# First-layer attention: the first three heads' projections and rotary embedding ahead of their share of the S5 table work

## Chip, cores and metric

One NeuronCore of a Trainium2 chip runs the whole program in one launch. The metric is the device time of one execution in microseconds. The kernel before was timed in three runs; their median is 2292.32 us.

## What is computed

Two transformer-like blocks of two layers each, on 256 latent and 256 context tokens of width 1024. The first layer of the first block is windowed attention with rotary embedding, 16 query heads and 4 key heads of width 128; the second is an S5 state-space mixer. All data are float32. What matters here, cut from the reference:

```python
pz = h @ w_in; pzc = hc @ w_in          # layer 0: q (16x128), k (4x128), v (4x128), z (2048)
q = rope_2d(q, row, col); k = rope_2d(k, row, col)      # latent tokens only
pr = softmax_with_sink(concat([s_win, s_ctx], -1), sink)
...
y_attention * silu(z) @ w_out            # end of layer 0
...
abar = exp(lam * dt); bbar = ((abar - 1) / lam)[..., None] * bmat    # layer 1: S5, two directions
hs = associative_scan(abar, bbar u);  y = einsum('btgp,gnp->btgn', hs, cmat).real
```

The S5 layer's input-independent tables (powers of `abar`, `bbar`, `cmat` in a transposed layout, and what is built from them) are computed by this kernel during the attention layer, as work beside the heads.

## The kernel before, in words

Every float32 matrix product is done as three passes (`mm3`, lines 197 to 202): each operand is split into a high part, rounded by ScalarE (`copy_a`, line 149), and a low part, the difference, mostly on VectorE (`sub`, line 152). A weight unit (`wunit`, line 204) is one 512 KB load on SyncE's queue into a ring of six staging tiles `st`, the high part on ScalarE and the low part on VectorE into a ring of three tiles `wl`.

`block1_l0` (line 622) makes the modulated inputs `hT`, the value projection of all heads, and then calls `l0_attention` (line 415). In it

- `heads(h)` (line 449) makes, for every fourth head, the key projection and its rope, and for each head the q projection with rope and the gate projection z. One projection is one weight unit and 8 times `mm3`, 24 matmuls, into one of three PSUM tiles `pa`. `rope` (line 431) reads that tile: ScalarE copies (line 149), VectorE differences (line 152), two matmuls with a rotation matrix (lines 437, 438), and products with cos and sin (line 158); only then is the tile `pa` free, for the projection that comes three later. The result is one tile `h` (a ring of 16, line 120), kept until the head's scores.
- `scores(h)` (line 461) and `values(h)` (line 506) are the attention of one head.
- `side` is a list of four generators: the S5 tables `s5_transposed` (line 763), the modulation `ada`, `s5_build_w` on GpSimd (line 951), `s5_build_v` on VectorE (line 901). One `next` does one step.

`s5_transposed` is driven in the lead alone, in 22 steps. Step 1 makes four transposes (line 768) and four VectorE copies. Step 2 is `s5_tables` (line 844): chains of small VectorE multiplications (`cmul`, lines 836 to 838; `three`, lines 841, 842), ScalarE copies into the tile `P` (line 867), and two `pwd` and five `apd` stores on GpSimd's queue. Steps 3 to 10 load the c matrices (two tiles `h` of 512 KB per real or imaginary part) and transpose them with 128-row matmuls (line 804), evacuated by VectorE and ScalarE in turn (lines 807 to 809) into four tiles `h`, which go to DRAM as `cbd` on GpSimd's queue. Steps 11 to 18 do the same for b, and steps 19 to 22 multiply b by the factor `qt` (lines 820 to 828) and store it.

The order on each engine's queue is not the order of the program: the framework plans it at compile time (line 2057, `schedule_with_timeline_sim=True`), taking on each engine the earliest instruction of the program that its plan has ready, and each engine then executes its queue strictly in that order. So the order of the program is a ranking.

Of the kernel before, what the change touches and what calls it, by code (L numbers as in the profile page):

```python
# [110 lines left out]
class Builder:  # L111
# [303 lines left out]
    def l0_attention(self, hT, vps, W, sink, negsink, Wo, gates, ada):  # L415
# [8 lines left out]
        def proj(n0):  # L424
            ps = self.pacc()
            w = self.w_ws(W, n0)
            for kt in range(8):
                self.mm3(ps, w[kt], (hT[kt][:, 0, :], hT[kt][:, 1, :]), kt == 0, kt == 7)
            return ps

        def rope(ps):
            hl = self.hslot(F32R)[:, :].rearrange("p (a b) -> p a b", a=2)
            pr = self.qslot(F32R)[:, :].rearrange("p (a b) -> p a b", a=2)
            self.split(pr, ps[:, :256])
            self.split(hl[:, :, 256:], ps[:, 256:])
            rq = self.pms()
            nc.tensor.matmul(rq[:, :256], self.rot, pr[:, 0, :], start=True, stop=False)
            nc.tensor.matmul(rq[:, :256], self.rot, pr[:, 1, :], start=False, stop=True)
            t = self.qslot()
            self.mul(t[:, :256], ps[:, :256], self.c["cos1"])  # L440
            self.mul(t[:, 256:], rq[:, :256], self.c["sin1"])
            self.add(t[:, :256], t[:, :256], t[:, 256:], self.off)
            self.split(hl[:, :, :256], t[:, :256], lo_eng=self.off)
            return hl
# [4 lines left out]
        def heads(h):  # L449

            g = h // 4
            if h % 4 == 0:
                Ks[g] = rope(proj(2048 + g * 128))
            q = rope(proj(h * 128))
            zps = proj(3072 + h * 128)
            th = self.qslot()
            nc.scalar.activation(th, zps, AF.Tanh, scale=0.5)
            self.stt(th, th, 1.0, zps, ALU.add, ALU.mult)
            pend[h] = [q, th]
# [136 lines left out]
        LEAD = 3  # L596
        side = [self.s5_transposed(), ada, self.s5_build_w(), self.s5_build_v()]
        for h in range(LEAD):
            for _ in range((2, 10, 10)[h]):
                next(side[0], None)  # L600
            heads(h)
        scores(0)
        for h in range(16):
            if h < 15:
# [1456 lines left out]
```

## Time and profile before

| what | value |
|---|---|
| median of three runs | 2292.32 us (2291.62 to 2294.66) |
| profiled execution, its own time | 2306.04 us |
| its span, first to last instruction | 2304.3 us |
| TensorE (PE) busy | 87% of the span |
| VectorE (DVE) / ScalarE (ACT) / GpSimd (POOL) busy | 62% / 38% / 32% |

All times of the trace are microseconds from the start of the span. Each engine's row in a timeline gives start, duration, engine, line of the code and operation, the tile written and the tiles read, and in brackets the idle time of the engine ahead of it and what ended it. The attention layer runs from about 57 to 700 us.

### The profile page before, as it was taken

The numbers are of one execution on the slowest core, as the hardware profiler recorded it, in microseconds if no ns is written. First come the engines' busy times: TensorE is split into PE (matmuls) and PEld (weight loads), VectorE is DVE, ScalarE is ACT, GpSimd is POOL, SyncE is SP. The second block draws the span as 40 slices with busy tenths as digits, with TensorE's granted clock in tenths as the row PEclk, the third lists the DMA queues.
The fourth block names the chain that finished last, engine by engine and source line by source line (L and its number), as shares of the span: only waits on it lengthen the run. The fifth ranks groups of instructions, "written<-read, shape, count | busy, mean of one in ns | idle before, by whom it ended". The sixth has DMA issues, their size and how long they took to land. (4 is left out here: it accounts for less than half of the span.)

```text
span 2304.3 us, 34637 instructions
## 1 busy us (share of the span) xinstructions
PE 2014.0 (87%) x13236; PEld 1587.5 (69%) x13236; DVE 1426.6 (62%) x2948; ACT 875.3 (38%) x1650; POOL 744.2 (32%) x498
## 2 busy tenths in 40 slices
PE   6697777999988878659998899999999989888998
PEld 3574555667767766647886565778888877557997
DVE  5788887766784867654656636553333476355556
ACT  2233233343534443443544243342222243334443
POOL 1686887900003201223442200121211513112334
PEclk9798877999999899779999879999999999788999
DMA  8566535554646666978675407433233225364663
GB/s 267 172 193 206 172 107 158 151 164 146 221 158 132 189 158 191 219 203 264 181 255 173 158 2 253 140 97 96 83 109 92 88 73 189 119 193 125 191 187 120
DMA packets 362775, 368.56 MB, mean 160 GB/s; under 512 B 27512, under 2 KB 291420, under 8 KB 362608
## 3 DMA queue, kind: packets, MB, share of 16 engines
q1 hardware_dynamic: 356048, 355.32, 51.7%
q0 software_dynamic: 2208, 6.29, 1.0%
q10 hardware_dynamic: 4352, 4.72, 0.6%
q8 instruction: 105, 1.72, 0.3%
q14 instruction: 62, 0.51, 0.1%
HBM read 319.62 MB, written 46.65 MB: 159 GB/s over the span
## 5 line engine op out<-in xcount | busy, mean ns | idle before, releaser
L149 ACT ACTIVATE wl<-st 128x1024 fp32r<-128x1024 f32 (+1 forms) x328 | 340.6, 1043 | 479.9 <-issue 177.6
L152 POOL TENSOR_TENSOR wl<-st,wl 128x1024 fp32r<-128x1024 f32 (+1 forms) x95 | 232.3, 2446 | 839.4 <-ACT wl L149 816.5
L152 DVE TENSOR_TENSOR wl<-st,wl 128x1024 fp32r<-128x1024 f32 (+1 forms) x233 | 312.0, 1341 | 242.5 <-ACT wl L149 240.8
L200 PE MATMUL pa<-h,wl 128*128 128x512 f32 (+1 forms) x1152 | 404.7, 354 | 13.9 <-ACT wl L149 6.5
L201 PE MATMUL pa<-h,wl 128*128 128x512 f32 (+1 forms) x1152 | 404.6, 352 | 0.0
L202 PE MATMUL pa<-h,wl 128*128 128x512 f32 (+1 forms) x1152 | 402.1, 351 | 1.1 <-DVE wl L152 1.1
L200 PEld LDWEIGHTS pa<-h,wl 128*128 128x128 f32 x1152 | 221.3, 193 | 49.7 <-ACT wl L149 8.3
L202 PEld LDWEIGHTS pa<-h,wl 128*128 128x128 f32 x1152 | 221.6, 193 | 31.0 <-DVE wl L152 1.7
L201 PEld LDWEIGHTS pa<-h,wl 128*128 128x128 f32 x1152 | 222.2, 193 | 27.5 <-issue 0.2
L201 PE MATMUL pa<-wl,h 128*128 128x512 f32 (+1 forms) x528 | 211.5, 401 | 11.2 <-DVE wl L152 9.8
L200 PE MATMUL pa<-wl,h 128*128 128x512 f32 (+1 forms) x528 | 206.0, 403 | 8.2 <-ACT h L149 4.1
L202 PE MATMUL pa<-wl,h 128*128 128x512 f32 (+1 forms) x528 | 203.2, 396 | 6.5 <-POOL h L152 5.6
L152 POOL TENSOR_TENSOR h<-q,h 128x256 fp32r<-128x256 f32 (+2 forms) x82 | 96.5, 1184 | 236.2 <-ACT h L149 162.3
L168 DVE SCALAR_TENSOR_TENSOR q<-q,pa 128x512 f32<-128x512 f32 (+1 forms) x104 | 59.0, 568 | 168.6 <-ACT q L1888 92.5
L149 ACT ACTIVATE h<-pm 128x512 f32<-128x512 f32 (+3 forms) x182 | 92.8, 546 | 153.7 <-PE pm L1556 38.9
L201 PE MATMUL pm<-wl,h 128*128 128x512 f32 (+1 forms) x376 | 146.7, 393 | 2.7 <-DVE wl L152 2.0
L299 PE MATMUL pf<-st,cs 128*32 128x512 f32 x576 | 97.0, 702 | 54.6 <-DMA st<-in_w_ada_dram 28.8
L202 PE MATMUL pm<-wl,h 128*128 128x512 f32 (+1 forms) x376 | 142.5, 391 | 0.0
L200 PE MATMUL pm<-wl,h 128*128 128x512 f32 (+1 forms) x376 | 140.1, 393 | 0.9 <-ACT wl L149 0.9
L201 PEld LDWEIGHTS pa<-wl,h 128*128 128x128 f32 x528 | 105.1, 199 | 38.0 <-DVE wl L152 11.5
L200 PEld LDWEIGHTS pa<-wl,h 128*128 128x128 f32 x528 | 104.1, 198 | 38.9 <-ACT h L149 8.5
L202 PEld LDWEIGHTS pa<-wl,h 128*128 128x128 f32 x528 | 103.6, 197 | 30.0 <-POOL h L152 6.4
(360 smaller groups left out, 3814.6 us busy)
## 6 DMA issues: line engine op xcount, KB each, us to landing
st<-in_w_ada_dram SPq DMA_DIRECT2D x96, 512.0 KB, 4.8
st<-in_ada_w_dram SPq DMA_DIRECT2D x48, 512.0 KB, 5.7
st<-in_w_ffn_gate_dram SPq DMA_DIRECT2D x44, 512.0 KB, 4.6
st<-in_w_ffn_up_dram SPq DMA_DIRECT2D x44, 512.0 KB, 3.9
st<-in_w_ffn_down_dram SPq DMA_DIRECT2D x44, 512.0 KB, 3.7
st<-in_attn_w_in_dram SPq DMA_DIRECT2D x40, 512.0 KB, 4.3
st<-in_w_out_dram SPq DMA_DIRECT2D x40, 512.0 KB, 4.0
wd<-w SPq DMA_DIRECT2D x64, 256.0 KB, 4.0
```

What stands on the lines that cost most here:

```text
L149: self.nc.scalar.activation(o, i, AF.Copy)
L152: return (eng or self.nc.vector).tensor_tensor(o, a, b, op=ALU.subtract)
L168: self.nc.vector.scalar_tensor_tensor(o, a, s, b, op0=op0, op1=op1)
L200: mm(o, w[0], x[0], start=start, stop=False)
L201: mm(o, w[0], x[1], start=False, stop=False)
L202: mm(o, w[1], x[0], start=False, stop=stop)
L299: mm = nc.tensor.matmul(ps[32 * q:32 * q + 32, :], self.cs[:, blk, kt, :, :], st[:, (q % 2) * 512:(q % 2 + 1) * 512], start=k0 == 0, stop= ...
```

## The change

In the loop over the first three heads, `heads(h)` stands ahead of that head's steps of `s5_transposed` (2, 10 and 10 of them) and no longer behind them. Nothing is added or removed.

```diff
         LEAD = 3
         side = [self.s5_transposed(), ada, self.s5_build_w(), self.s5_build_v()]
         for h in range(LEAD):
+            heads(h)
             for _ in range((2, 10, 10)[h]):
                 next(side[0], None)
-            heads(h)
         scores(0)
```

## Rows read from the trace of the kernel before

**Rows 1.** The page: the span, and the busy time of each engine.
```profile
span 2304.3 us, 34637 instructions
PE 2014.0 (87%) x13236; PEld 1587.5 (69%) x13236; DVE 1426.6 (62%) x2948; ACT 875.3 (38%) x1650; POOL 744.2 (32%) x498
```
**Rows 2.** Stretches A:B, their length, busy us of each engine, granted clock, DMA.
```profile
75.00:400.00 325.00, 256.57 (x1491) 185.98 (x1490) 280.61 (x358) 106.00 (x238) 242.21 (x166) 0.83 0.54 167
400.00:640.00 240.00, 234.51 (x1513) 173.39 (x1512) 172.03 (x282) 103.69 (x221) 58.12 (x40) 0.97 0.54 174
72.00:126.00 54.00, 40.31 (x200) 30.06 (x199) 53.33 (x74) 15.71 (x27) 32.22 (x27) 0.84 0.54 163
126.00:150.00 24.00, 24.00 (x210) 20.73 (x209) 17.20 (x38) 10.99 (x29) 21.93 (x19) 1.00 0.92 289
150.00:215.00 65.00, 48.14 (x253) 31.96 (x251) 64.41 (x71) 17.41 (x43) 52.15 (x33) 0.90 0.58 176
...
102.00:110.00 8.00, 1.40 (x4) 0.63 (x3) 8.00 (x10) 1.32 (x3) 5.24 (x5) 0.50 0.80 260
```
**Rows 3.** Timeline of PE in the lead.
```profile
76.55 0.50 PE L200 MATMUL pa<-h,wl 128*128 128x512 f32 x1
...
93.48 1.06 PE L299 MATMUL pf<-st,cs 128*32 128x512 f32 x8
101.63 0.58 PE L437 MATMUL pm<-q,rot 128*128 128x256 f32 x1 [7.09 <-ACT q L149]
104.05 0.58 PE L438 MATMUL pm<-q,rot 128*128 128x256 f32 x1 [1.84 <-DVE q L152]
...
109.97 0.77 PE L200 MATMUL pa<-h,wl 128*128 128x512 f32 x1 [4.65 <-DVE q L158]
...
113.51 0.39 PE L202 MATMUL pa<-h,wl 128*128 128x512 f32 x1
```
**Rows 4.** Timeline of ACT in the lead.
```profile
98.63 2.55 ACT L149 ACTIVATE h<-h 64x512 f32<-64x512 f32 x4 [5.79 <-DVE h L155]
101.20 0.38 ACT L149 ACTIVATE q<-pa 128x256 fp32r<-128x256 f32 x1
```
**Rows 5.** Timeline of DVE.
```profile
58.45 0.28 DVE L163 TENSOR_SCALAR a<-pm 128x128 f32<-128x128 f32 x1
...
72.09 1.58 DVE L152 TENSOR_TENSOR wl<-st,wl 128x1024 fp32r<-128x1024 f32 x1 [13.36 <-ACT wl L149]
...
79.05 1.27 DVE L841 COPY h<-h 128x128 f32<-128x128 f32 x1
...
86.89 0.21 DVE L841 COPY h<-h 128x128 f32<-128x128 f32 x1
...
109.42 0.41 DVE L158 TENSOR_TENSOR q<-pa,cst 128x256 f32<-128x256 f32 x1
109.75 0.41 DVE L155 TENSOR_TENSOR h<-h 128x256 f32<-128x256 f32 x1
...
359.93 1.53 DVE L155 TENSOR_TENSOR q<-q 128x256 f32<-128x256 f32 x1
```
**Rows 6.** POOL: its first S5 product on the timeline, and all products of `w`.
```profile
60.95 1.51 POOL L158 TENSOR_TENSOR w<-bs,qg 128x512 f32<-128x512 f32 x1 [20.47 <-DMA bs<-in_s_b_im_dram]
...
L155 POOL TENSOR_TENSOR w<-w,wd x64: 1267/1590/2170, 65.1 to 456.5; 128x512 f32<-128x512 f32 x64
```
**Rows 7.** SyncE's queue: the loads of b.
```profile
127.31 1.04 SPq L146 DMA_DIRECT2D h<-in_s_b_re_dram  x2
...
139.24 5.68 SPq L146 DMA_DIRECT2D h<-in_s_b_im_dram  x2
```
**Rows 8.** PE: the transposing matmuls of c and b.
```profile
122.26 4.97 PE L804 MATMUL pm<-cst,h 128*64 128x128 f32 x64
...
132.70 7.33 PE L804 MATMUL pm<-cst,h 128*64 128x128 f32 x96
```

## The prediction

> **What bounds the kernel now.** The page first, for the scale: TensorE is busy in 87% of the span, VectorE in 62% [rows 1]. A change to the first three heads must be read from its own stretch, so next the stretches. From 400 to 640 us PE is busy in 234.5 of 240 us and VectorE in 172: there PE sets the pace, and whatever earlier stretches lose or win passes on to the end one for one. From 75 to 400 us it is the reverse: VectorE is busy in 280.6 of 325 us and PE in 256.6 [rows 2]. The lead, where the change works, is the fullest part of that: 53.3 of 54 us on VectorE from 72 to 126, then 17.2 of 24, then 64.4 of 65 [rows 2]. The reader should see that PE's idle time in the lead is mostly a consequence: it waits for a VectorE that has no time to spare, except in the 24 us from 126 to 150, where PE is the full one (24.0 of 24) and VectorE has 6.8 us over.
>
> Then the timeline of PE. From 76.55 to 93.48 it makes 72 matmuls, the projections K0, q0 and z0, at 0.235 us each. Then, but for 1.06 us of other work, it stands: 7.09 us until ScalarE has split K0, 1.84 us for a VectorE difference, 4.65 us until VectorE's product with the cosine gives back K0's tile `pa`, for which q1's projection waits [rows 3]. Together 13.6 us. ScalarE's timeline says why: K0's projection ended about 82.2 (76.55 plus 24 times 0.235), but its split runs at 101.20, behind four copies of the S5 table `P` which themselves waited 5.79 us for VectorE's table chain [rows 4]. The cosine product comes at 109.42 [rows 5]. So the ranking of tables ahead of heads is really felt: rope K0 stands some 20 us behind table work in two in-order queues.
>
> **The change, part by part.** No work is added or removed; every term is a displacement.
>
> Heads(0) ahead of two steps of tables. K0's split no longer ranks behind the copies of `P`, and its six VectorE operations at 0.41 us [rows 5], 2.5 us, no longer rank behind the chain. They would run soon after 82.2, and q1 would find its tile free at 93.5. On PE this takes away up to 13.6 us of standing. The granted clock also fell to 0.50 in 102 to 110, its 1.2 GHz level, and a matmul at 109.97 took 0.77 us where one at 113.51 took 0.39 [rows 2, 3]; the 3.5 us between them would be 1.8 at the full clock, so PE's side could give 15.4 us at most.
>
> What VectorE lets through of that. The same table, rope and weight operations are still due before scores(0), and VectorE is full in 72 to 126 and in 150 to 215 [rows 2]. PE running ahead lets VectorE start rope and weight work earlier but shortens none of it. What it can fill is the 6.8 us that VectorE has over in 126 to 150: there PE, at work on projections and the c and b transposes at once, made it wait; with q1 and z1 out of the way earlier that wait goes. The bounds of the gain are 0 (the hole stays) and 15.4 us (all of PE's standing goes for good, which needs holes elsewhere: from 75 to 400 us VectorE has 44.4 in all [rows 2]). I take 6.8, the hole itself, as it is the nearest row, in the lead and on the engine that is full.
>
> The moved steps' other instructions. Step 1's four transposes and copies, done by 58.7 now, have VectorE's hole from there to 72.09 as cover, 13.4 us [rows 5], and being ready early they should stay in it: 0; without that cover they cost under 2 us. The table stores on POOL's queue (two `pwd`, five `apd`) get later by the 2.5 us of each rope that passes them; what is queued behind them is POOL's product stream, which runs to 456.5 us [rows 6] and which no head waits for: 0. The c and b loads on SyncE's queue (four tiles each) now rank behind the weight loads of heads(1) and heads(2); on PE the 256 transposing matmuls they feed have projections to run beside: 0 for the queue itself, but see the third rival. The b products and their `cbd` stores rank behind heads(2), by two weight differences and one rope; the only readers of `cbd`, the loads of `s5_build_v`, rank behind values(0) in both versions. VectorE's total up to scores(0) stays as it is, so 0 for the order alone, with the b products still the last work ahead of scores(0). ScalarE is busy in 15.7 of 54 us [rows 2]: 0.
>
> The products on VectorE and POOL touch each other. The same small copy took 1.27 us at 79.05, beside POOL's products, and 0.21 us at 86.89 [rows 5]; rope's addition took 0.41 at 109.75 and the same form 1.53 at 359.93 [rows 5]. I take no change of the sum, as the table operations that change places with rope are of the kind that is stretched too. The Trainium skill, "SBUF — State Buffer", section "Summary: rules for kernel authors", says that a VectorE operation with two SBUF inputs and a GpSimd operation that reads SBUF block each other whole, and to schedule whichever is off the critical path; by that rule the change puts ropes into POOL's busiest stretch, and only the ropes' price would count, which the fourth rival works out from the rows.
>
> The sum against the profiled execution: 2306.0 us less 6.8 is 2299.2. That execution is 13.7 us above the median of the three runs (2292.3), and its span is 1.7 below its own time. The forecast in terms of the median is 2292.3 less 6.8, or 2285.5; I say 2286.
>
> **The rivals.** First, nothing comes of it: VectorE stays full, PE's 13.6 us turn up again ahead of the b products and scores(0), where it already has only 48.1 of 65 us of work [rows 2]. For it: VectorE's 53.3 of 54. The same time comes out if the change does not do what it says, since the planner ranks and does not obey: POOL's first S5 product runs at 60.95 [rows 6], though the program has it behind values(0). Against it: K0's split truly stood behind the `P` copies. Time: 2292.
>
> Second, the larger gain: PE stays ahead, and the rest of VectorE's 44.4 us of holes up to 400 us takes up what the lead could not. Then 15.4 us go and the time is 2277. Against it: PE can run ahead by three `pa` tiles only, and scores and values follow VectorE.
>
> Third, slower: the ring of 16 tiles `h` becomes the bound. The b loads go out at 127.31, just when the first 64 transposing matmuls, of c's real part, have ended at 127.23 and given back two tiles [rows 7, 8]: the ring is full now. With q1 and q2 held from earlier on, the b loads would wait for the next two tiles, those of c's imaginary part, free after 64 of the 96 matmuls from 132.70 on, 132.70 + 64 x 0.0764 = 137.6 [rows 8]. That is 10.3 us later for the loads, for the b products behind them and for scores(0) behind those; it decides from the point where the displaced ropes and tables no longer fill VectorE meanwhile. Nothing gained and 10.3 lost is 2302.6. For it: the imaginary b load already takes 5.68 us to issue [rows 7]. Against it: c may start earlier when PE is ahead, and VectorE has its displaced table work to do meanwhile.
>
> Fourth, the ropes pay for POOL: four ropes (K0, q0, q1, q2) with two SBUF-only operations each, stretched by 1.53 less 0.41, cost 8 x 1.12 = 9.0 us, of which the gain of 6.8 covers most: 2294.5. By the skill's rule above this is the price of the change; rows of rope at 0.41 us in the lead speak against its full size.
>
> **How the numbers follow.** About 0.2%, 4.6 us, is what a measurement of this kernel can tell from no change. The forecast at 2286 has a chance of 0.34, the larger gain 0.11; nothing 0.20 and the ropes beside POOL 0.08, both within 4.6 us; the full ring 0.27. That gives faster 0.45, same 0.28, slower 0.27. Cases of both signs hold most of the chance; the likeliest one's own range is 2282 to 2290, from half as much again to a third of the term. The range reaches to the larger gain's 2277 and nearly to the ring's full price: 2277 to 2302, which leaves out about half of the first and a third of the second, some 15 in 100.
>
> **What would show it.** Right: K0's split on ScalarE runs within a few us of 82 and ahead of the second `P` copies; PE has no hole of 7 us between 93 and 102, and q1 follows z0 directly; VectorE stays full up to 150 and on, with its 6.8 us gone; scores(0) come some 7 us earlier, and PE's idle time from 75 to 400 us, 68.4 now, is smaller by as much. Wrong: the same sum of PE's idle time in that stretch in other places (the first rival); b loads later than 127 with VectorE idle ahead of the b products (the third); rope's additions at 1.2 us or more in the lead (the fourth). If the stretch up to 400 us keeps its time and the total still moves, the plan has changed further down, and the reasoning here does not reach it.

## The result, and the profile after

The change made the kernel slower: 2308.3 us, median of four runs, against 2291.97 us for the kernel before beside it, a ratio of 1.0067 with a 95% interval of 1.0046 to 1.0088. That is 16.3 us slower, where the forecast had some 6 us faster, and 6 us above the range's end. The page of the changed kernel:

```profile
span 2309.4 us, 34623 instructions
...
PE 2001.0 (87%) x13236; PEld 1582.4 (69%) x13236; DVE 1428.1 (62%) x2948; ACT 876.1 (38%) x1650; POOL 748.5 (32%) x498
```

The work is the same as in [rows 1]. The two spans differ by 5.1 us only, since the profiled execution of before is 13.7 us above its median, as the prediction's sum says. So the spans are no measure here; I read the stage the change is in. Its first and last marks are the first scores (line 472) and the last statistics of the attention's output (line 593). These are groups of instructions by line: count, shortest/mean/longest ns, first start and last end. Kernel before:

```profile
L472 PE MATMUL pm<-lowneg,identb x16: 229/230/331, 166.3 to 645.4; 128*128 128x128 bf16 x16
...
L593 DVE BATCH_NORM_STATS2 bn<-h x8: 680/690/695, 684.3 to 696.8; 128x6 f32<-128x512 f32 x8
```

Changed kernel:

```profile
L472 PE MATMUL pm<-lowneg,identb x16: 229/230/330, 195.1 to 661.8; 128*128 128x128 bf16 x16
...
L593 DVE BATCH_NORM_STATS2 bn<-h x8: 639/684/695, 698.0 to 710.8; 128x6 f32<-128x512 f32 x8
```

The first scores come 28.8 us later (195.1 less 166.3), the end of the attention 14.0 us later (710.8 less 696.8), near the 16.3 of the medians. In this pair of profiles more than the kernel's loss is made before the first scores, and about half of it comes back on the way.

Now the lead itself, the stretch from about 57 us to the first scores. The stretches of the changed kernel (columns as in [rows 2]):

```profile
57.00:100.00 43.00, 39.16 (x167) 31.14 (x166) 19.63 (x27) 14.18 (x24) 39.58 (x27) 0.96 0.60 165
...
100.00:150.00 50.00, 31.04 (x172) 22.68 (x171) 48.96 (x67) 11.89 (x19) 33.84 (x28) 0.80 0.60 186
126.00:150.00 24.00, 18.01 (x114) 14.65 (x114) 23.54 (x34) 4.48 (x8) 16.51 (x15) 0.80 0.75 237
150.00:215.00 65.00, 42.74 (x296) 34.66 (x294) 50.38 (x74) 15.46 (x44) 48.45 (x36) 0.84 0.68 212
...
75.00:400.00 325.00, 229.19 (x1434) 171.80 (x1435) 276.38 (x348) 100.08 (x229) 251.35 (x170) 0.83 0.52 162
...
57.00:215.00 158.00, 112.93 (x632) 88.49 (x630) 118.98 (x166) 41.53 (x87) 121.86 (x89) 0.86 0.63 191
```

and two of the kernel before that [rows 2] do not have:

```profile
57.00:100.00 43.00, 31.94 (x134) 24.24 (x132) 29.04 (x39) 12.95 (x21) 28.94 (x22) 0.88 0.54 153
...
57.00:215.00 158.00, 121.85 (x693) 89.97 (x691) 136.40 (x186) 48.00 (x105) 117.35 (x86) 0.88 0.63 192
```

Between 57 and 100 us PE is busier than before, 39.2 us against 31.9, and yet the lead is lost. Over 57 to 215 VectorE does 119.0 us of work instead of 136.4: the engine that was full in the lead stood 17.4 us longer, and not all of it in one place. Up to 100 us it does 9.4 us less (19.6 instead of 29.0). From 100 to 150 it does 6.0 more (49.0 instead of 43.0, which is 136.40 less 29.04 and less the 64.41 of [rows 2]), nearly all of that in 126 to 150, where it is now busy in 23.5 of 24 us and was in 17.2. From 150 to 215 it does 14.0 less (50.4 instead of 64.4). So there are two losses, one before 100 us and a larger one after 150.

The first loss, on three timelines. PE of the changed kernel:

```profile
74.88 0.50 PE L200 MATMUL pa<-h,wl 128*128 128x512 f32 x1
...
92.18 0.38 PE L768 MATMUL pm<-cst,ab 128*128 128x128 f32 x2
92.40 0.38 PE L768 MATMUL pm<-cst,qg 128*128 128x128 f32 x2
92.54 0.48 PE L200 MATMUL pa<-h,wl 128*128 128x512 f32 x1
...
124.89 0.58 PE L437 MATMUL pm<-q,rot 128*128 128x256 f32 x1 [6.73 <-ACT q L149]
...
158.41 9.01 PE L804 MATMUL pm<-cst,h 128*64 128x128 f32 x64 [7.20 <-DMA h<-in_s_c_im_dram]
```

PE of the kernel before, the same four transposes:

```profile
56.99 0.40 PE L768 MATMUL pm<-cst,ab 128*128 128x128 f32 x2
57.22 0.38 PE L768 MATMUL pm<-cst,qg 128*128 128x128 f32 x2
```

VectorE of the changed kernel:

```profile
70.44 1.81 DVE L152 TENSOR_TENSOR wl<-st,wl 128x1024 fp32r<-128x1024 f32 x1 [11.99 <-ACT wl L149]
77.27 1.23 DVE L152 TENSOR_TENSOR wl<-st,wl 128x1024 fp32r<-128x1024 f32 x1 [5.02 <-ACT wl L149]
81.23 0.42 DVE L152 TENSOR_TENSOR q<-pa,q 128x256 fp32r<-128x256 f32 x1 [2.73 <-ACT q L149]
...
89.63 1.52 DVE L152 TENSOR_TENSOR h<-q,h 128x256 fp32r<-128x256 f32 x1
...
92.61 1.34 DVE L155 TENSOR_TENSOR q<-q 128x256 f32<-128x256 f32 x1
93.88 0.41 DVE L770 COPY q<-pm 128x256 f32<-128x256 f32 x1
...
95.40 1.16 DVE L858 COPY h<-a 128x128 f32<-128x128 f32 x1
...
165.26 0.38 DVE L809 COPY h<-pm 128x128 f32<-128x128 f32 x1 [9.12 <-ACT h L149]
```

and of the kernel before, the first operation of the table chain (the serial run of small operations in step 2):

```profile
73.60 1.31 DVE L858 COPY h<-a 128x128 f32<-128x128 f32 x1
```

The four transposes of step 1 ran at 57 us before. In the changed kernel they stand in PE's queue at 92.18, behind all 72 matmuls of K0, q0 and z0 (74.88 to 92.3). Everything in step 2 starts from them: the copies at 93.88, the chain's first operation at 95.40 instead of 73.60, 21.8 us later. In the meantime VectorE stood for 11.99, 5.02 and 2.73 us. The first of these is nothing new, it was 13.36 us before [rows 5]; the other two lie where the chain ran before. From its first operation to the end of the second copies of `P` the chain took 27.6 us before (73.60 to 101.18, [rows 4]) and takes 29.0 here (95.40 to 124.43), as ScalarE shows, whose copies of `P` close its two halves:

```profile
80.81 0.39 ACT L149 ACTIVATE q<-pa 128x256 fp32r<-128x256 f32 x1 [3.57 <-PE pa L202]
...
112.66 2.55 ACT L149 ACTIVATE h<-h 64x512 f32<-64x512 f32 x4 [13.15 <-DVE h L155]
...
121.88 2.55 ACT L149 ACTIVATE h<-h 64x512 f32<-64x512 f32 x4 [4.65 <-DVE h L155]
124.45 0.38 ACT L149 ACTIVATE q<-pa 128x256 fp32r<-128x256 f32 x1
```

K0's split is early now, 80.81 instead of 101.20 [rows 4]. But the second copies of `P` are at 121.88 instead of 98.63, and right behind them, at 124.45, stands q1's split, as K0's stood before. PE's hole of 7.09 us [rows 3] is there again as 6.73 us at 124.89; it has gone from K0 to q1.

The second loss. The loads of c and b on SyncE's queue come later:

```profile
132.01 1.67 SPq L146 DMA_DIRECT2D h<-in_s_c_re_dram  x2
...
152.97 0.35 SPq L146 DMA_DIRECT2D st<-in_ada_w_dram  x1
153.36 0.90 SPq L146 DMA_DIRECT2D h<-in_s_c_im_dram  x2
154.36 1.09 SPq L146 DMA_DIRECT2D h<-in_s_b_re_dram  x2
...
176.44 1.51 SPq L146 DMA_DIRECT2D h<-in_s_b_im_dram  x2
```

b's real part leaves at 154.36 instead of 127.31, its imaginary part at 176.44 instead of 139.24 [rows 7]. PE's transposes of c's imaginary part, whose loads left at 153.36, come at 158.41 after a wait of 7.20 us for them, and behind PE VectorE stands 9.12 us in the middle of c's evacuation, ahead of 165.26. The loads of c's imaginary part leave directly behind a weight load (152.97 and 0.35 us), b's real part directly behind c's. So what they waited for was their turn in SyncE's queue. Whether that is the late chain's doing or the loads' new rank behind heads(1) and heads(2), the first experiment tells.

### The profile page after: what moved, and what is told of

The parts are those of the page before. It is cut to its first block, busy times and chain, and to the rows that moved or that the text cites. A ratio compares the mean times of both kernels' runs of the same rounds, so it can differ in the third digit from the quotient of the medians.

```text
span 2309.4 us, 34623 instructions
## 1 busy us (share of the span) xinstructions
PE 2001.0 (87%) x13236; PEld 1582.4 (69%) x13236; DVE 1428.1 (62%) x2948; ACT 876.1 (38%) x1650; POOL 748.5 (32%) x498
## 5 line engine op out<-in xcount | busy, mean ns | idle before, releaser
L200 PE MATMUL pa<-h,wl 128*128 128x512 f32 (+1 forms) x1152 | 403.9, 353 | 17.4 <-DVE q L158 12.1
L299 PE MATMUL pf<-st,cs 128*32 128x512 f32 x576 | 93.1, 670 | 53.5 <-DMA st<-in_w_ada_dram 27.4
```

What stands on the lines that cost most here:

```text
L200: mm(o, w[0], x[0], start=start, stop=False)
L299: mm = nc.tensor.matmul(ps[32 * q:32 * q + 32, :], self.cs[:, blk, kt, :, :], st[:, (q % 2) * 512:(q % 2 + 1) * 512], start=k0 == 0, stop= ...
```

## The experiments

Two theories went into the runs. The **lead theory**: the late table chain costs what is seen before the first scores, and the kernel's time follows. The **plan theory**: any edit of the program's order redraws the planned order of the later heads too, and that alone moves the time.

**Halves of the change.** Heads(0) alone ahead of its two steps:

```diff
         for h in range(LEAD):
+            if h == 0:
+                heads(h)
             for _ in range((2, 10, 10)[h]):
                 next(side[0], None)
-            heads(h)
+            if h > 0:
+                heads(h)
```

> Only heads(0) goes ahead of its two steps (transposes and tables); heads(1) and heads(2) stay behind theirs. Theory of the late chain: the serial table chain on VectorE starts when the ropes of K0 and q0 are through, near 95 us instead of 73.6, and everything that ends in scores(0) and the first v product follows; then this edit alone gives nearly all of the change, some 2305 to 2310 us (before: 2292), with scores(0) near 190 us or later. Theory of the full ring (c and b loads behind heads(1) and heads(2)): this edit alone costs nothing, 2289 to 2295.

Measured: 2302.43 us, ratio 1.0041 (1.0022 to 1.0061), between the two expectations. The transposes run at 93.5, the chain starts at 95.8, the first scores at 180.3:

```profile
L472 PE MATMUL pm<-lowneg,identb x16: 229/230/331, 180.3 to 649.7; 128*128 128x128 bf16 x16
```
```profile
121.66 0.84 SPq L146 DMA_DIRECT2D h<-in_s_c_re_dram  x2
...
135.20 2.81 SPq L146 DMA_DIRECT2D h<-in_s_c_im_dram  x2
```

This half alone has the late chain, as late as in the whole change, and 14 of the 29 us. The other 15 need heads(1) and heads(2) ahead of their steps as well. With the same chain start, c's loads leave 10 and 18 us earlier here than in the whole change (121.66 against 132.01, 135.20 against 153.36), in which three more loads of projection weights stand ahead of c's first, and VectorE does 59.0 us of work in 150 to 215 here, against 50.4 there. So the second loss is not the chain's alone.

Heads(1) and heads(2) alone ahead of theirs (the same edit with `h > 0` and `h == 0` exchanged):

> Only heads(1) and heads(2) go ahead of their ten steps each; the transposes and tables stay ahead of heads(0). Late chain: the chain starts at 73.6 us as before and the time is that of before, 2288 to 2296. Full ring or queue order: the b loads leave later than 127 us with VectorE idle ahead of the b products, and most of the loss is here, 2300 to 2308.

Measured: 2309.56 us, ratio 1.0078 (1.0057 to 1.01), above both expectations. Here the chain starts at 73.9 as before, b's real part leaves at 134.45 and the first scores are 4 us late only, and yet this kernel is as slow as the whole change:

```profile
L472 PE MATMUL pm<-lowneg,identb x16: 229/231/330, 170.6 to 659.6; 128*128 128x128 bf16 x16
...
L593 DVE BATCH_NORM_STATS2 bn<-h x8: 679/688/696, 699.1 to 711.7; 128x6 f32<-128x512 f32 x8
```

Its 4 us at the first scores have shrunk to 0.5 by head 4 and are 15 at the end of the attention; 8 of them arise between heads 4 and 5, whose first scores lie 44 us apart instead of 36. The lead theory does not reach this, and the two halves do not add up to the whole (0.41% and 0.78% against 0.67%). Heads(1) alone ahead of its ten steps:

> Only heads(1) goes ahead of its ten steps; heads(0) and heads(2) stay behind theirs. If the loss of the edit with heads(1) and heads(2) sits in the c loads that rank behind heads(1) (c transposes began at 128.6 us there and at 122.3 before), it is here: 2300 to 2310. If it was the redrawn order of the later heads, this edit draws another one: anything from 2285 to 2308, and scores(0) within 6 us of 166 in either case.

Measured: 2305.24 us, ratio 1.0048 (1.0028 to 1.0068), chain at 71.2, first scores at 168.0, attention's end at 704.4. The same picture, half the size.

**Where in the lead.** The changed order with step 1 (the transposes) ahead of heads(0), the tables of step 2 behind it:

```diff
+        next(side[0])
         for h in range(LEAD):
             heads(h)
-            for _ in range((2, 10, 10)[h]):
+            for _ in range((1, 10, 10)[h]):
                 next(side[0], None)
```

> As the changed kernel, but the four transposes and copies of step 1 stay ahead of heads(0); only the tables of step 2 rank behind it. If what delayed the chain was that the transposes were queued on PE behind the 72 matmuls of K0, q0 and z0, the tables now find their inputs at 58 us and fill VectorE's holes between 58 and 81 us (20 us in the changed kernel): chain start before 75 us, 2285 to 2294. If the ranking of the tables behind the ropes and weights is what counts, the time stays at 2304 to 2310.

Measured: 2302.13 us, ratio 1.0042 (1.0023 to 1.0061). The transposes are back at 58.2, but the chain's first operation comes at 88.7, its `P` copies at 107.7 and 117.2, the first scores at 186.5. The time is just below what was expected if the tables' rank is what counts. So the transposes' place on PE is 7 of the chain's 22 us; the rest comes with step 2's own rank behind heads(0).

The other way round: the order of before, but the two table steps ranked inside the value projection, the first behind the first half of the modulated inputs, the second behind the second half:

```diff
             hT += self.to_fm(X, grp, kts=range(k, k + 4))

+            if k == 4:
+                next(self.s5t)
             if k == 0:
+                self.s5t = self.s5_transposed()
+                next(self.s5t)
                 vps = self.acc4(4)
...
-        side = [self.s5_transposed(), ada, self.s5_build_w(), self.s5_build_v()]
+        side = [self.s5t, ada, self.s5_build_w(), self.s5_build_v()]
         for h in range(LEAD):
-            for _ in range((2, 10, 10)[h]):
+            for _ in range((0, 10, 10)[h]):
```

> The other way round: the kernel before, with step 1 after the first half of the modulated inputs and step 2 after the second half, ahead of the second half of the value projection; heads as before. Late chain: an earlier chain fills VectorE's 13.4 us hole of 59 to 72 us, scores(0) come up to 13 us earlier than 165.6 and the time falls to 2279 to 2287. If the lead is bound by anything else (PE, loads, the ring), it stays at 2289 to 2296; if the table operations ahead of K0's weights now delay PE, it is 2296 or more.

Measured: 2299.17 us, ratio 1.0022 (0.9995 to 1.005): no difference that can be told. The chain starts at 57.0 and the first scores come at 153.0, 13 us earlier than before; by head 7 (first scores 410 against 419) 9 us of that are left, at the attention's end (695.4) 1.4. The expectation held for the first scores and failed for the time.

And both: the tables early and the heads first.

```diff
         for h in range(LEAD):
-            for _ in range((2, 10, 10)[h]):
-                next(side[0], None)
             heads(h)
+            for _ in range((0, 10, 10)[h]):
+                next(side[0], None)
```

> The three heads ahead of their steps as in the change, but the transposes and tables already between and behind the two halves of the modulated inputs, so the table chain begins near 57 us. Late chain: what remains of the change does no harm in the lead; scores(0) at 150 to 165 us. With the lead's 10 us or so passing on as in the other early kernel, 2283 to 2300; if heads ahead of c and b steps is a loss in itself, 2303 to 2310 again.

Measured: 2284.72 us, ratio 0.9967 (0.9952 to 0.9981), faster than the kernel before and, by its ratio, than the changed one. It differs from the changed kernel in the place of two steps only. Groups by line and the stretch 57 to 215 of it:

```profile
L472 PE MATMUL pm<-lowneg,identb x16: 229/230/330, 165.1 to 635.5; 128*128 128x128 bf16 x16
...
L593 DVE BATCH_NORM_STATS2 bn<-h x8: 671/684/695, 674.9 to 687.4; 128x6 f32<-128x512 f32 x8
```
```profile
57.00:215.00 158.00, 128.06 (x710) 95.85 (x711) 140.80 (x190) 52.22 (x113) 125.07 (x91) 0.87 0.64 196
```

Its chain, on VectorE and on ScalarE:

```profile
56.09 0.22 DVE L862 COPY h<-a 128x128 f32<-128x128 f32 x1
```
```profile
68.52 2.55 ACT L149 ACTIVATE h<-h 64x512 f32<-64x512 f32 x4 [6.00 <-DVE h L155]
81.01 2.55 ACT L149 ACTIVATE h<-h 64x512 f32<-64x512 f32 x4 [5.79 <-DVE h L155]
92.71 0.39 ACT L149 ACTIVATE q<-pa 128x256 fp32r<-128x256 f32 x1 [5.97 <-PE pa L202]
```

The chain starts at 56.09 in the hole VectorE had, the last copies of `P` are out by 83.6, and K0's split waits for its projection (92.71, released by PE), no longer for a table. VectorE does 140.8 us of work up to 215. Over the eight kernels with ten and ten steps behind the tables, VectorE's work in 57 to 215 and the first scores go together nearly in order:

| kernel | VectorE busy in 57 to 215, us | first scores, us |
|---|---|---|
| before's order, tables early | 147.1 | 153.0 |
| heads first, tables early | 140.8 | 165.1 |
| heads 1 and 2 first | 137.5 | 170.6 |
| before | 136.4 | 166.3 |
| heads 1 first | 134.8 | 168.0 |
| step 1 first | 124.8 | 186.5 |
| heads 0 first | 124.6 | 180.3 |
| the change | 119.0 | 195.1 |

This says where the lead went, but not what the kernel's time is. Heads first costs 12 us at the first scores with early tables (165.1 against 153.0) and 29 with the tables where they were (195.1 against 166.3). At the attention's end it is 8 us won in the one case (687.4 against 695.4) and 14 lost in the other (710.8 against 696.8), and the ratios go the same way as these.

**The plan theory.** Two edits that leave the tables and the order of the kernel before as they are: its steps dealt 2, 9, 11 and 2, 12, 8 to the three heads, so that one or two steps of the c and b work change heads.

```diff
-            for _ in range((2, 10, 10)[h]):
+            for _ in range((2, 9, 11)[h]):
```

> The kernel before with the steps dealt 2, 9 and 11 over the three heads and the heads still behind their steps: the lead is that of before but for one step of b passing heads(1)'s successors, while the planned order of all later heads comes out differently. If the time is set by the lead (the place of the table chain), this stays within 4 us of 2292. If the plan of the later heads is drawn anew by any edit and that is worth as much as the lead, it can differ by 5 to 17 us, to either side, with scores(0) within 3 us of 166.

> The kernel before with the steps dealt 2, 12 and 8, heads behind their steps: two steps of b earlier, otherwise the lead of before. Lead theory: within 4 us of 2292. Theory of the redrawn plan: 5 to 17 us off, to either side, with scores(0) near 166.

Measured: 2303.34 and 2302.17 us, ratios 1.0038 (1.0024 to 1.0053) and 1.0039 (1.0025 to 1.0054). First scores at 166.0 and 159.9, not later than before, and both some 9 us slower. So an edit of next to nothing costs 0.4%, more than half of what the change cost. One kernel against one kernel is therefore no verdict on an order. The same two deals went to the changed order and to the order with early tables:

> The order of the changed kernel, with the table steps dealt 2, 9, 11 instead of 2, 10, 10: same lead, another plan further down. Lead theory (the tables that start some 20 us later cost some 7 us wherever the later heads are placed, and a redrawn plan moves the rest by about as much): first scores at 190 to 200 us, time 2300 to 2315. Rival, the redrawn plan alone decides: time anywhere from 2290 to 2312, around 2302 like the two null edits, and this one and the next on both sides of it.

> The order of the changed kernel, dealt 2, 12, 8. Lead theory: first scores at 185 to 200 us, time 2300 to 2315. Rival, the redrawn plan alone: 2290 to 2312, around 2302.

> The changed order with the first two table steps inside the value projection, as in the run that beat both, dealt 9, 11 behind: first scores near 165 us as there. Lead theory: 2280 to 2297, below both kernels of the changed order whose tables start at 95 us. Rival, the redrawn plan alone (2284.7 was a lucky draw): around 2302, and as likely above the two kernels before as below.

> The same with 12, 8 behind. Lead theory: 2280 to 2297. Rival, the redrawn plan alone: around 2302.

Measured, as ratios to the kernel before on the same chip, with the attention's end of each profile. The columns are the steps of heads(1) and heads(2):

| order | 10, 10 | 9, 11 | 12, 8 | mean | attention's end, us |
|---|---|---|---|---|---|
| before | 1 | 1.0038 | 1.0039 | 1.0026 | 696.8, 697.6, 697.1 |
| the change | 1.0067 | 1.0074 (1.0051 to 1.0097) | 1.0148 (1.0115 to 1.0181) | 1.0096 | 710.8, 716.8, 727.2 |
| tables early, heads first | 0.9967 | 0.9958 (0.994 to 0.9975) | 1.0009 (0.9985 to 1.0032) | 0.9978 | 687.4, 685.9, 696.4 |

Against before's order with the same deal, the changed order is slower in all three, by 0.36 to 1.09%, the mean 0.70% or 16 us. Against the changed order, the one with early tables is faster in all three, by 1.0 to 1.4%, on average 1.17% or 27 us. The ratios of the two heads-first orders do not overlap (0.9958 to 1.0009 against 1.0067 to 1.0148): the plan theory, by which they should have mingled around 2302, falls as the whole explanation. It stays as a second effect, of up to 0.8% between deals of one order. So it is shown, on three kernels each, that with the heads first the tables' early place is worth some 1.2%. That the late chain is what makes the change slower than before is the likeliest reading and not shown: heads(1) and heads(2) ahead cost as much, 0.78%, with the chain where it was, and heads(0) ahead cost 0.41%, no more than the null edits. Two numbers missed what I gave them by the lead theory: the 12, 8 deal of the changed order is at 2331.1, above 2315, and that of the early tables at 2299.25, 2 above 2297.

## Why the prediction was wrong

**What bounds the lead** was read rightly for the kernel before: VectorE, with PE's holes a consequence. PE got 7 us busier in 57 to 100 and the kernel slower. But the change took VectorE's place as the full engine away from it in two stretches, and the prediction took it as given. That later stretches pass a loss on held, nearly, only from 400 us on: head 7 is 19 us late, head 15 is 16; between the first and third heads 29 had become 20.

**Heads(0) ahead of the tables.** The first signs came true: K0's split at 80.81, no hole on PE from 93 to 102, q1's projection right behind z0's at 92.54. VectorE's hole in 126 to 150, the term of 6.8 us, was filled too, to 6.3 us (23.54 busy against 17.20). It brought nothing forward, because VectorE stood elsewhere: 9.4 us more before 100 and 14.0 more after 150. PE's idle time from 75 to 400 us, which was to shrink by some 7 us, grew by 27.4, from 68.4 to 95.8.

**The step that failed** is "Step 1's four transposes and copies, done by 58.7 now, have VectorE's hole from there to 72.09 as cover, 13.4 us [rows 5], and being ready early they should stay in it: 0". They did not stay in it: ranked behind heads(0), they were queued at 92 and 94 us. I priced their own 2 us and looked at the hole on VectorE, but not at who waits for them: the whole serial chain of step 2. In its place belongs: the chain starts 21.8 us later, VectorE does 9.4 us less up to 100, the stand behind the `P` copies goes over to q1, and with heads(0) alone ahead the first scores come 14.0 us later. A second term failed beside it, the c and b loads behind the weight loads of heads(1) and heads(2), "0 for the queue itself" because PE was to have projections to run beside: PE stood 7.20 us for c's imaginary part and VectorE 9.12, and with both displacements the first scores come 28.8 us later. Putting step 1 back gives only 7 of the chain's 22 us, so step 2's own rank counts as well, and with it fall the words "VectorE's total up to scores(0) stays as it is, so 0 for the order alone". No operation was added, but a serial chain and loads that start late leave holes that no total shows. How much of the 16.3 us of the whole kernel is due to these two terms stays open, as the experiments on the halves say. The table stores, priced as later "by the 2.5 us of each rope", went with the chain: the first `pwd` store left at 115.50 instead of 92.05, the last `apd` at 154.63 instead of 129.44.

**The rivals.** The third, slower to 2302.6, came nearest in time and sign, and its marks are there (b loads later than 127, VectorE idle ahead of the b products). Its reason, the full ring of tiles `h`, is not shown: the late loads leave right behind what stands ahead of them in SyncE's queue. So they did before, where b's at 127.31 followed c's imaginary part (126.23 and 1.03 us), and that two tiles came free at 127.23 may be chance. Late loads alone do not settle the first scores either. In the fastest kernel c's and b's leave later than before as well, and the first scores do not come later:

```profile
117.00 1.79 SPq L146 DMA_DIRECT2D h<-in_s_c_re_dram  x2
...
130.46 0.90 SPq L146 DMA_DIRECT2D h<-in_s_b_re_dram  x2
```

The fourth, ropes that pay for POOL, is there in good part: the difference at 89.63 took 1.52 us and the addition at 92.61 took 1.34. The 0.41 us that the prediction set against them, at 109.75 [rows 5], belong to the table chain (tiles `h`) and not to a rope, but K0's addition before took as long:

```profile
110.41 0.41 DVE L155 TENSOR_TENSOR q<-q 128x256 f32<-128x256 f32 x1
```

The rope differences of the lead, 57 to 215 us, before and in the changed kernel:

```profile
L152 DVE TENSOR_TENSOR h<-q,h 128x256 fp32r<-128x256 f32 x4 | 1.7, 415 | 0.2 <-ACT h L149 0.2
```
```profile
L152 DVE TENSOR_TENSOR h<-q,h 128x256 fp32r<-128x256 f32 x4 | 7.1, 1779 | 0.0
```

With the four additions (2.0 us before, 3.4 now) the ropes cost 6.8 us more, near the rival's 9.0. The rule on two-input VectorE operations in the Trainium skill, "SBUF — State Buffer", section "Summary: rules for kernel authors", agrees in direction. Table operations of the same kind got shorter meanwhile (ten products `h<-h` of 128x256 took 8.1 us instead of 10.9), as the prediction assumed, so what is left of this price is smaller and not measured.

**Further down.** The prediction named as its limit that the plan might change there; it does, and the chances gave it no weight. With equal deals the order itself costs 0.36 to 1.09%. What stays open: where the two null edits lose their 9 us (their attention ends within 1 us of before's, and single executions differ by more: 29 runs of the kernel before on one chip went from 2284.28 to 2305.67), why heads(1) and heads(2) ahead cost 0.78% on their own and not with early tables, and why 13 us won at the first scores (tables early, heads last) are all but gone 540 us later. No run here settles these.

## What to carry to other kernels

Before a step is ranked behind other work, ask for its longest serial successor, not for its own length: two steps ranked behind one head's projections put off a chain of 28 us by 22, and with it work of the engine that was full. Ask the same of loads: a load ranked behind others leaves when its turn in the queue comes, and the engine that was to have work beside it may have none by then. Where both things are wanted early, look for an idle stretch further up for the head of the chain; here moving two steps into the value projection made the same heads-first order 1.0 to 1.4% faster. And where a planner lays out the queues, compare an order with another over several near-null variants of each, as one variant against another of the same order moved this kernel by up to 0.8%.
